# Residual with features on partitions from the output projection to gate and up, and cross attention as one pipeline

## The chip, the core and the metric

The kernel runs on one core of a Trainium2 chip. The metric is the time of one execution on the device, in microseconds (us). Before the change the median of 3 runs is 2864.52 us (2863.82 to 2865.51).

## What is computed

One transformer block in float32 on 2048 tokens of 1024 features, with three kinds of causal attention side by side, cross attention to a memory of 256 tokens, and a gated feed-forward layer:

```python
def _rmsnorm(x, g):
    xf = x.astype(jnp.float32)
    y = xf * lax.rsqrt(jnp.mean(xf * xf, axis=-1, keepdims=True) + EPS)
    return (y * g.astype(jnp.float32)).astype(x.dtype)
...
        y = jnp.concatenate([_rmsnorm(ya, ga), _rmsnorm(yb, gb), _rmsnorm(yc, gc)], axis=-1)
        x = x + y @ w_o[l]
        x = x + _cross(_rmsnorm(x, norm_cross[l]), _rmsnorm(mem, norm_mem[l]),
                       w_cq[l], w_ckv[l], w_co[l])
        h = _rmsnorm(x, norm_ffn[l])
        gate, up = jnp.split(h @ w_gu[l], 2, axis=-1)
        x = x + (jax.nn.silu(gate) * up) @ w_down[l]
```

`_cross` makes queries (4 heads of 128) from the normalised residual, scores them against the memory's keys, takes the softmax, and projects the weighted values back with w_co. The hidden width of the feed-forward layer is 2816, that is 22 blocks of 128.

## The kernel before

The program runs its stages one after the other: projections, the three attentions, output projection, cross attention, gate and up, down projection. Every operand of a large matmul is split into a high and a low part (tiles with h and l at the end), and one product is three matmuls, high by high, high by low and low by high (`mm3`, the matmul is on line 94). The instructions are written by a program whose scheduler puts those of each engine into a fixed order by a simulated timeline when the kernel is built; every engine then runs its own list strictly in that order, and a waiting instruction holds back all behind it. ScalarE's list also issues DMA transfers, as does SyncE's.

The residual lies with tokens on partitions. TensorE multiplies along the partitions, so an operand that is to be summed over features has to be transposed first (by matmuls with an identity matrix, four 128x128 pieces into one PSUM tile); ScalarE then evacuates the high part and VectorE the low part.

- The output projection (lines 889 to 957) goes over 8 pieces of 256 tokens. `load_y` loads two tiles `yt` of 128 tokens of the attention result over ScalarE's queue (line 923), normalises them into `yht` (`rms_rows`, squares on line 119), and transposes them (`transpose_split`: line 142 on TensorE, 146 on ScalarE, 147 on VectorE). w_o is loaded in 8 blocks over SyncE's queue and cast (lines 907 to 909). Per 128 tokens the residual piece is stored to `s_x2`, and normalised to `s_h2` (16 tiles each).
- Cross attention (lines 960 to 1065) loads `s_h2` in four chunks of 512 tokens and transposes it (128 transposes, line 142, tile `ht`). For each chunk and head come queries `cq`, scores and softmax `soft` (tiles `cs`, `cp`), the weighted values `val`, and `outp` (tile `co`), which adds to the residual, stores it to `s_x3`, normalises it and stores that to `s_h3`. The softmax of the next head runs beside the values of the one before; a chunk's `outp` runs inside the next chunk.
- Gate and up (lines 1071 to 1246) uses a seven-product scheme for 2x2 block matrices, in two halves of 1024 tokens by 22 blocks of hidden width. `blocks` forms sums of the operands on GpSimd, and `turn` (lines 1127 to 1129) transposes the 7 x 4 operands of a half: 112 transposes for each half, 224 in all. Weight sums and splits (lines 1158 to 1161, 1103 and 1104) run for each of the 22 blocks.

The pools of the three stages are separate, in SBUF and in PSUM.

Of the kernel before, what the change touches and what calls it, by code (L numbers as in the profile page):

```python
# [8 lines left out]
F32 = mybir.dt.float32  # L9
# [24 lines left out]
def kernel(ctx: ExitStack, tc: tile.TileContext, a: dict, out: bass.AP, dbg=None):  # L34
# [26 lines left out]
    s_x2 = [scratch([CH, D], f"s_x2_{c}") for c in range(NCH)]  # L61
    s_x3 = [scratch([CH, D], f"s_x3_{c}") for c in range(NCH)]
    s_h2 = [scratch([CH, D], f"s_h2_{c}") for c in range(NCH)]
    s_h3 = [scratch([CH, D], f"s_h3_{c}") for c in range(NCH)]
# [15 lines left out]
    G_MIX, G_OUT, G_CROSS, G_MEM, G_Q, G_KV = 0, 8, 16, 24, 32, 34  # L80
# [807 lines left out]
    late = ExitStack()  # L888
    mp = pool(late, "mkv", side="right")
    wqp = pool(late, "cwq", side="right")  # L890

    mp.tile([P, 24], F32, name="rpad")
    mkT = [mp.tile([P, 4, MEM], F32R, name=f"mkT{i}") for i in range(2)]
    mv = [mp.tile([P, 2, 512], F32R, name=f"mv{i}") for i in range(2)]
    with ExitStack() as es:
        xp = pool(es, "ox")
        wp = pool(es, "ow")
        hp = pool(es, "oh")
        rp = pool(es, "or")
        pp = pool(es, "opp", space=PSUM)  # L900

        def loadw(src, tag, bufs, k):
            n = src.shape[1]
            th = wp.tile([P, n], F32R, name="wh_", tag=tag + "h", bufs=bufs)
            tl = wp.tile([P, n], F32R, name="wl_", tag=tag + "l", bufs=bufs)
            r = wp.tile([P, n], F32, name="wraw", tag="wraw", bufs=2)
            nc.sync.dma_start(r, src)
            nc.vector.tensor_copy(th, r)
            (nc.gpsimd if k % 2 else nc.vector).tensor_sub(tl, r, f32(th))
            return th, tl  # L910

        def load_wq(k):
            th, tl = wqp.tile([P, 512], F32R, name=f"wqh{k}"), wqp.tile([P, 512], F32R, name=f"wql{k}")
            r = wp.tile([P, 512], F32, name="wraw", tag="wraw", bufs=2)
            nc.scalar.dma_start(r, a["w_cq"][0][k * P:(k + 1) * P, :])
            split(r, th, tl)
            return th, tl

        def load_y(c):
            hts = []  # L920
            for t in range(2):
                yt = xp.tile([P, D], F32, name="yt", tag="yt", bufs=3)
                nc.scalar.dma_start(yt, s_y[c // 2][(c % 2) * 256 + t * P:(c % 2) * 256 + (t + 1) * P, :])
                ht = xp.tile([P, D], F32, name="yht", tag="ht", bufs=4)
                rms_rows(yt, [(0, 512), (512, 768), (768, 1024)], ht, sp)
                hts.append(ht)
            return transpose_split(hts, G_OUT, hp, pp, "yT", 16, pbufs=2)

        y0 = load_y(0)
        wo = [loadw(a["w_o"][0][k * P:(k + 1) * P, :], "wo", 8, k) for k in range(KT)]  # L930
        yT = {0: y0}
        wq = []
        for c in range(8):
            hh, hl = yT.pop(c)
            if c + 1 < 8:
                yT[c + 1] = load_y(c + 1)
            if c == 3:
                for i in range(2):
                    nc.sync.dma_start(f32(mkT[i]), s_ck[i])
                    nc.sync.dma_start(f32(mv[i]), s_cv[i])  # L940
            if c >= 4:
                wq += [load_wq(2 * c - 8), load_wq(2 * c - 7)]
            for t in range(2):
                ts = slice(t * P, (t + 1) * P)
                r0 = c * 256 + t * P
                rr = slice(r0 % CH, r0 % CH + P)
                xt = rp.tile([P, D], F32, name="xt", tag="xt", bufs=3)
# [12 lines left out]
    with ExitStack() as es:  # L960
# [15 lines left out]
        def turn(hts):  # L976
            return transpose_split(hts, G_CROSS, hp, pp, "xT", 8)
# [468 lines left out]
```

## Time and profile before

| | |
|---|---|
| median of 3 runs | 2864.52 us |
| profiled execution | 2859.2 us |
| its span in the trace | 2857.5 us |
| TensorE, mean granted clock | .988 of full speed |
| output projection, about | 1008 to 1207 us |
| cross attention, about | 1207 to 1484 us |
| gate and up, about | 1484 to 2385 us |

The span is the time between the first and the last instruction in the trace, and the execution's own time is 1.7 us longer. Engines are named PE (TensorE), DVE (VectorE), ACT (ScalarE), POOL (GpSimd) and SP (SyncE); PEld is TensorE's weight load, which overlaps the matmuls. "Busy" of TensorE is a sum over pipelined matmuls whose ends are modelled, so a mean duration is no pitch: the pitch is a stretch of time divided by the matmuls in it.

### The profile page before, as it was taken

What the parts mean: (1) busy time and instruction counts of PE and PEld (TensorE: products, weight loads), DVE (VectorE), ACT (ScalarE), POOL (GpSimd) and SP (SyncE); (2) the same over time, 40 slices, a digit from 0 to 9 for tenths busy, and PEclk for the clock granted to TensorE, in tenths of its full rate; (3) what the DMA queues carried; (4) which work ended last, traced back from release to release, by engine and by line L of the source; (5) the groups of instructions that cost most, each with busy time, mean ns of one, the idle gap of its engine ahead of it and who ended that gap; (6) DMA issues with size and microseconds to landing.
All of it is one profiled execution on the core that took longest, in us unless ns stands there. A gap on an engine that the chain in (4) does not pass through costs nothing. (4 is left out here: it accounts for less than half of the span.)

```text
span 2857.5 us, 40439 instructions
## 1 busy us (share of the span) xinstructions
PE 2762.3 (97%) x13537; PEld 2290.1 (80%) x13537; DVE 1860.7 (65%) x3677; ACT 1306.7 (46%) x2816; POOL 1239.6 (43%) x991
## 2 busy tenths in 40 slices
PE   8999999999999999999989999999999997999996
PEld 7888888888888878778867888887788885888885
DVE  6446458887777764456666665566666663677778
ACT  5225219998776734344444333334333334333335
POOL 3132253332111120010026766666666667579854
PEclk9999999999999999999999999999999998999998
DMA  7755457433342174533253333233333333445434
GB/s 260 261 174 210 177 198 214 123 105 113 114 121 74 50 254 169 181 115 133 97 213 123 110 104 103 90 106 105 108 106 109 100 104 118 130 155 184 133 96 144
DMA packets 300448, 398.72 MB, mean 140 GB/s; under 512 B 39168, under 2 KB 174592, under 8 KB 300240
## 3 DMA queue, kind: packets, MB, share of 16 engines
q1 hardware_dynamic: 291168, 372.79, 39.5%
q10 hardware_dynamic: 9072, 23.35, 2.2%
q8 instruction: 107, 1.75, 0.2%
q14 instruction: 101, 0.83, 0.1%
HBM read 258.54 MB, written 137.51 MB: 139 GB/s over the span
## 5 line engine op out<-in xcount | busy, mean ns | idle before, releaser
L1375 DVE TENSOR_TENSOR acc<-dn,acc 128x512 f32<-128x512 f32 x352 | 226.0, 682 | 69.6 <-PE dn L1368 67.4
L772 POOL TENSOR_TENSOR ptl<-pf,pth 128x512 fp32r<-128x512 f32 (+3 forms) x111 | 109.9, 990 | 361.7 <-ACT pth L771 237.3
L1368 PE MATMUL dn<-wdh,gdh 128*128 128x512 f32 x616 | 238.0, 394 | 18.9 <-ACT acc L1373 15.8
L1104 POOL TENSOR_TENSOR awl<-s,awh 128x512 fp32r<-128x512 f32 x132 | 193.6, 1467 | 131.9 <-ACT awh L1103 123.5
L1368 PE MATMUL dn<-wdl,gdh 128*128 128x512 f32 x616 | 240.4, 391 | 1.2 <-POOL wdl L1267 1.2
L1368 PE MATMUL dn<-wdh,gdl 128*128 128x512 f32 x616 | 236.5, 393 | 3.4 <-POOL gdl L1267 3.4
L1103 ACT CAST awh<-s 128x512 fp32r<-128x512 f32 x176 | 109.1, 621 | 251.5 <-PE p L94 246.9
L723 ACT ACTIVATE pt<-pt,m 128x640 f32<-128x640 f32 (+4 forms) x192 | 206.1, 1076 | 32.9 <-DVE pt L709 29.6
L763 PE MATMUL tp<-ident,pt 128*128 128x128 f32 x1368 | 217.5, 274 | 3.7 <-ACT pt L723 2.3
L775 DVE TENSOR_TENSOR ptl<-tp,pth 128x512 fp32r<-128x512 f32 (+3 forms) x321 | 183.2, 587 | 43.4 <-ACT pth L774 41.2
L1265 ACT CAST gdh<-graw 128x512 fp32r<-128x512 f32 x154 | 95.5, 622 | 247.9 <-PE dn L1368 128.2
L763 PEld LDWEIGHTS tp<-ident,pt 128*128 128x128 f32 x1368 | 165.5, 140 | 30.7 <-ACT pt L723 3.2
L774 ACT CAST pth<-tp 128x512 fp32r<-128x512 f32 (+3 forms) x321 | 159.4, 518 | 43.2 <-PE tp L763 39.7
L1267 POOL TENSOR_TENSOR gdl<-graw,gdh 128x512 fp32r<-128x512 f32 x98 | 137.2, 1412 | 77.9 <-ACT gdh L1265 54.8
L789 PE MATMUL pv<-ptl,va 128*128 128x512 f32 (+3 forms) x432 | 166.2, 391 | 0.0
L703 PE MATMUL s<-ka,qa 128*128 128x512 f32 (+8 forms) x432 | 162.7, 380 | 1.9 <-DVE r L561 0.6
L789 PE MATMUL pv<-pth,va 128*128 128x512 f32 (+3 forms) x432 | 160.6, 374 | 1.9 <-ACT pth L774 1.9
L1103 ACT CAST awh<-graw 128x512 fp32r<-128x512 f32 x132 | 81.5, 619 | 166.4 <-PE p L94 107.9
L1368 PEld LDWEIGHTS dn<-wdh,gdh 128*128 128x128 f32 x616 | 116.6, 189 | 48.1 <-ACT acc L1373 17.6
L1368 PEld LDWEIGHTS dn<-wdh,gdl 128*128 128x128 f32 x616 | 116.7, 190 | 28.3 <-POOL gdl L1267 3.8
L1368 PEld LDWEIGHTS dn<-wdl,gdh 128*128 128x128 f32 x616 | 116.4, 189 | 25.3 <-POOL wdl L1267 1.6
L187 POOL TENSOR_TENSOR wl<-wr,wh 128x512 fp32r<-128x512 f32 (+1 forms) x36 | 50.5, 1405 | 135.2 <-DVE wh L185 112.2
(470 smaller groups left out, 8331.9 us busy)
## 6 DMA issues: line engine op xcount, KB each, us to landing
graw<-in_w_gu_dram SPq DMA_DIRECT2D x88, 512.0 KB
graw<-s_g SPq DMA_DIRECT2D x154, 256.0 KB
s_g<-pair SPq DMA_DIRECT2D x66, 256.0 KB
s_h<-xh SPq DMA_DIRECT2D x32, 512.0 KB
ht<-s_h SPq DMA_DIRECT2D x32, 512.0 KB
wr<-in_w_in_dram SPq DMA_DIRECT2D x48, 256.0 KB
s_g<-u SPq DMA_DIRECT2D x44, 256.0 KB
draw<-in_w_down_dram SPq DMA_DIRECT2D x22, 512.0 KB
```

The costliest lines, as they stand in the source:

```text
L703: nc.tensor.matmul(dst, l, r, start=j == 0, stop=j == len(seq) - 1)
L723: nc.scalar.activation(v.pt[:, 0:nk * P], v.pt[:, 0:nk * P], AF.Exp, bias=v.prev, scale=-1.0, accum_out=u.l[:, t:t + 1])
L763: nc.tensor.transpose(ps[:, t * P:(t + 1) * P], u.p[t][:, o:o + P], ident)
L772: nc.gpsimd.tensor_sub(lo[:, cs], pf[:, cs], f32(hi[:, cs]))
L774: nc.scalar.copy(hi[:, cs], ps[:, cs])
L775: nc.vector.tensor_sub(lo[:, cs], ps[:, cs], f32(hi[:, cs]))
L789: nc.tensor.matmul(st.ps[:, cs], l, r[:, cs], start=b == blocks[0] and j == 0, stop=b == blocks[-1] and j == len(seq) - 1)
L1103: nc.scalar.copy(tiles[0], raw)
L1104: (nc.gpsimd if k else nc.vector).tensor_sub(tiles[1], raw, f32(tiles[0]))
L1267: (nc.vector if cnt[0] % 3 == 0 else nc.gpsimd).tensor_sub(t[1], x, f32(t[0]))
L1368: nc.tensor.matmul(ps[t], l[:, ts], r, start=p == chain[0][0] and i == 0, stop=i == len(seq) - 1, skip_group_check=True)
L1375: nc.vector.tensor_add(x, ps[t], x)
```

## The change

The residual now lies with features on partitions (tiles of 128 features by 512 tokens) from the output projection to gate and up.

- Output projection: w_o is the stationary operand and the transposed attention result the moving one. It goes over four chunks of 512 tokens; all 16 blocks of w_o stay in SBUF. The residual's own input is read from `xT`, the transposed input. The squares of the new residual are summed on ScalarE and GpSimd (`squares`), turned into a sum per token by four matmuls with one column of ones (`rms_cols`), and used as a scale on the scores (`rsc`); norm_cross is folded into w_cq (`load_wq`). There is no `s_h2` any more. In the last chunk `x_steps(0)` reloads the first chunk and splits it.
- Cross attention: one loop over 16 units (chunk and head), with the queries of the next unit and the values of the last inside it. `x_steps` splits the reloaded residual without a transpose (copy on ScalarE, subtraction on VectorE or GpSimd). `outp` writes 128 features at a time. `rows` transposes the new residual back to tokens on partitions for `s_x3` (128 transposes). `norm1` and `norm2` spread the factor of each token over the partitions (four matmuls of `ones` with a diagonal tile `dg`), and multiply (8 operations on VectorE per chunk); the result is stored to `s_h3` with features on partitions.
- Gate and up: `turn` has no transposes: copy on ScalarE, subtraction on VectorE (every fourth on GpSimd), from SBUF. The first two products of the first block are started before the last chunk's norm (`begun`).
- The three stages share one PSUM pool (6 buffers for sums, 2 for transposes).

The diff, cut to its core:

```diff
+    def squares(st, p, m, x):
+        if m == 0:
+            st[0] = p.tile([P, CH], F32, name="ssum", tag="ssum", bufs=1)
+            nc.scalar.activation(st[0], x, AF.Square)
+        else:
+            sq = p.tile([P, CH], F32, name="sq", tag="sq", bufs=2)
+            nc.scalar.activation(sq, x, AF.Square)
+            nc.gpsimd.tensor_add(st[0], st[0], sq)
+
+    def rms_cols(st):
+        ps = pp.tile([P, CH], F32, name="rc", tag="tp", bufs=2)
+        for t in range(4):
+            nc.tensor.matmul(ps[:, t:t + 1], st[0][:, t * P:(t + 1) * P], ones[:, 0:1], start=True, stop=True)
...
+    def x_steps(c, p, tag, bufs):
...
+            nc.sync.dma_start(raw, s_x2[c][k])
+            th, tl = ft()
+            nc.scalar.copy(th, raw)
+            (nc.gpsimd if k % 3 == 1 else nc.vector).tensor_sub(tl, raw, f32(th))
...
         def load_wq(k):
...
+            nc.sync.dma_start(r, a["w_cq"][0][k * P:(k + 1) * P, :])
+            g = gains[:, G_CROSS + k:G_CROSS + k + 1]
+            nc.scalar.mul(th, r, g)
+            nc.vector.scalar_tensor_tensor(out=tl, in0=r, scalar=g, in1=f32(th), op0=ALU.mult, op1=ALU.subtract)
...
         def load_y(c):
             hts = []
-            for t in range(2):
-                yt = xp.tile([P, D], F32, name="yt", tag="yt", bufs=3)
...
+            for t in range(4):
+                yt = xp.tile([P, D], F32, name="yt", tag="yt", bufs=5)
+                nc.scalar.dma_start(yt, s_y[c][t * P:(t + 1) * P, :])
+                junk = xp.tile([P, D], BF16, name="junk", tag="junk", bufs=1)
+                rms_rows(yt, [(0, 512), (512, 768), (768, 1024)], yt, sp, junk=junk)
+                hts.append(yt)
...
+                    for i in range(4):
+                        ms = slice(i * P, (i + 1) * P)
+                        mm3(ps[i], [((wo[k, n][0][:, ms], wo[k, n][1][:, ms]), y[k])], start=k == 0, stop=k == KT - 1)
...
+                for i in range(4):
+                    nc.vector.tensor_add(xt[i], ps[i], xt[i])
+                    nc.sync.dma_start(s_x2[c][4 * n + i], xt[i])
+                    squares(st, rp, 4 * n + i, xt[i])
...
+    def norm2(c, x3, dg):
+        ps = pp.tile([P, CH], F32, name="tp", tag="tp", bufs=2)
+        for t in range(4):
+            nc.tensor.matmul(ps[:, t * P:(t + 1) * P], ones, dg[:, t, :], start=True, stop=True)
+        rb = lp.tile([P, CH], F32, name="rb", tag="sq", bufs=2)
+        nc.scalar.copy(rb, ps)
+        for m in range(KT):
+            nc.vector.scalar_tensor_tensor(out=x3[m], in0=x3[m], scalar=gains[:, G_FFN + m:G_FFN + m + 1], in1=rb,
+                                           op0=ALU.mult, op1=ALU.mult)
+            nc.sync.dma_start(s_h3[c][m], x3[m])
...
+    for u in range(16):
+        c, h = divmod(u, 4)
...
+            def turn(n, raw):
                 B[n] = [bt(n, j) for j in range(4)]
                 for j in range(4):
-                    ps = pp.tile([P, CH], F32, name="tp", tag="tp", bufs=2)
-                    for t in range(4):
-                        nc.tensor.transpose(ps[:, t * P:(t + 1) * P], rows[t][:, j * P:(j + 1) * P], ident)
-                    nc.scalar.copy(B[n][j][0], ps)
-                    nc.vector.tensor_sub(B[n][j][1], ps, f32(B[n][j][0]))
+                    nc.scalar.copy(B[n][j][0], raw[j])
+                    (nc.gpsimd if j % 4 == 3 else nc.vector).tensor_sub(B[n][j][1], raw[j], f32(B[n][j][0]))
...
+        for m in range(KT):
+            outp(3, oT, m, x3, st)
+            if m:
+                rows(3, m - 1, x3)
+            if m % 2 == 0 and begin:
+                begin.pop(0)()
+        begun = [w0, acc(), acc()]
+        block(begun[1], w0[0], B["11"])
+        rows(3, 7, x3)
+        dg = norm1(st)
+        block(begun[2], w0[1], B["t1"])
+        norm2(3, x3, dg)
```

What this does to the order of the instructions is shown at two places. The first is ScalarE at the end of attention and the start of the output projection, before; `pth` and `osb` belong to attention, `yt` are the loads, `trh` the evacuated operands:

```order
L923 DMA yt_13112<-s_y0_124 128x1024
L774 CAST pth_12845<-tp_12843 128x128
L923 DMA yt_13134<-s_y0_124 128x1024
L923 DMA yt_13260<-s_y0_124 128x1024
...
L119 ACTIVATE yht_13114,rms_ss_13115<-yt_13112 128x512
...
L771 CAST pth_13044<-tp_13042 128x128
L109 ACTIVATE rms_rs_13289<-rms_rs_13289 128x3
L794 COPY osb_13068<-pv_12931 128x512
L923 DMA yt_13732<-s_y1_125 128x1024
L146 ACTIVATE trh_13159<-tr_ps_13156,gains_315 128x256
```

The same place with the change (`fth` are the evacuated operands, `wqh` the scaled parts of w_cq):

```order
L770 CAST pth_13096<-tp_13094 128x128
L970 DMA yt_13174<-s_y0_124 128x1024
L970 DMA yt_13196<-s_y0_124 128x1024
L970 DMA yt_13218<-s_y0_124 128x1024
L793 COPY osb_13120<-pv_12983 128x512
L970 DMA yt_13240<-s_y0_124 128x1024
L118 ACTIVATE junk_13176,rms_ss_13177<-yt_13174 128x512
...
L118 ACTIVATE junk_13396,rms_ss_13397<-yt_13394 128x512
...
L982 ACTIVATE fth_13273<-tp_13268,gains_367 128x512
...
L962 ACTIVATE wqh0_14388<-wraw_14390,gains_367 128x512
```

The four loads of the first chunk moved from in front of attention's last casts to behind the last of them, and the squares of five tiles now stand between that cast and the first evacuated operand.

The second place is VectorE at the start of gate and up, before; `xh` is the last chunk's normalised residual, `b` tiles are the operands of the products:

```order
L1038 SCALAR_TENSOR_TENSOR xh_17538<-x3_17507,rms_rs_17541,hgain_15203 128x1024
L1033 TENSOR_TENSOR x3_17552<-co_17568,x3_17552 128x512
L107 TENSOR_SCALAR rms_nt_17587<-rms_ss_17584 128x1
L1129 TENSOR_TENSOR b11_0l_17653<-tp_17660,b11_0h_17652 128x512
L1129 TENSOR_TENSOR b11_1l_17655<-tp_17667,b11_1h_17654 128x512
...
L1038 SCALAR_TENSOR_TENSOR xh_17583<-x3_17552,rms_rs_17586,hgain_15203 128x1024
L1129 TENSOR_TENSOR b11_2l_17657<-tp_17674,b11_2h_17656 128x512
```

The same place with the change (`s1` to `s4` are weight sums of the second block, `rb` the spread factor):

```order
L1098 TENSOR_TENSOR x3_17792<-mm_17794,x3_17792 128x512
L1258 TENSOR_TENSOR s1_18077<-graw_18075 128x512
...
L1261 TENSOR_TENSOR s4_18080<-graw_18073,s2_18078 128x512
L924 COPY rms_ss_17846<-rc_17841 128x4
...
L1116 TENSOR_SCALAR dg_17857<-ident_357,rms_rs_17848 128x128 x4
L1126 SCALAR_TENSOR_TENSOR x3_17568<-x3_17568,gains_367,rb_17879 128x512
...
L1126 SCALAR_TENSOR_TENSOR x3_17792<-x3_17792,gains_367,rb_17879 128x512
L1230 TENSOR_TENSOR b21_0l_17907<-ht_17500,b21_0h_17906 128x512
L1230 TENSOR_TENSOR b21_1l_17909<-ht_17502,b21_1h_17908 128x512
```

The operands of the first two products (`b11`, `bt1`) moved in front of the last residual addition; those of the third (`b21`) stand behind the whole norm, and read SBUF (`ht`) where they read PSUM (`tp`) before.

## Rows read from the trace of the kernel before

**Rows 1.** Page, busy time of each engine, share of the span and instructions:

```profile
PE 2762.3 (97%) x13537; PEld 2290.1 (80%) x13537; DVE 1860.7 (65%) x3677; ACT 1306.7 (46%) x2816; POOL 1239.6 (43%) x991
```

**Rows 2.** Stretches: length, busy (instructions) of PE, PEld, DVE, ACT, POOL; clock; DMA share; GB/s:

```profile
1008.30:1206.80 198.50, 192.96 (x902) 156.01 (x902) 105.82 (x297) 73.70 (x241) 19.97 (x12) 1.00 0.54 196
1206.80:1484.20 277.40, 263.79 (x1313) 214.01 (x1312) 174.75 (x449) 117.92 (x296) 23.95 (x14) 0.97 0.40 146
1484.20:1600.00 115.80, 109.47 (x519) 86.17 (x518) 76.58 (x93) 47.44 (x84) 77.28 (x55) 1.00 0.34 119
1700.00:1815.80 115.80, 115.80 (x500) 93.85 (x500) 70.22 (x77) 38.40 (x65) 75.32 (x54) 1.00 0.32 103
1900.00:2015.80 115.80, 112.45 (x530) 90.22 (x529) 78.00 (x89) 45.47 (x80) 76.57 (x56) 0.99 0.32 108
```

**Rows 3.** The last three stretches, matmuls of line 94 alone:

```profile
1484.20:1600.00 115.80, 101.12 (x405) 73.84 (x404) 1.00 0.34 119
1700.00:1815.80 115.80, 115.80 (x500) 93.85 (x500) 1.00 0.32 103
1900.00:2015.80 115.80, 104.34 (x420) 77.58 (x419) 0.99 0.32 108
```

**Rows 4.** A stretch of the output projection: matmuls (L94), then transposes (L142):

```profile
1100.00:1200.00 100.00, 100.00 (x404) 72.88 (x403) 1.00 0.48 176
...
1100.00:1200.00 100.00, 12.92 (x68) 9.55 (x68) 1.00 0.48 176
```

**Rows 5.** Timeline of ScalarE and its DMA queue: start, length, instruction, [wait before]:

```profile
983.49 0.33 ACTq L923 DMA_DIRECT2D yt<-s_y  x1
...
987.34 0.63 ACT L119 ACTIVATE yht<-yt 128x512 f32<-128x512 f32 x1
...
988.67 0.19 ACT L119 ACTIVATION_READ_ACCUMULATOR yht<-yt 128x1 f32 x1
...
992.08 0.66 ACT L106 ACTIVATE rms_rs<-rms_ss,epsc 128x1 f32<-128x1 f32 x3
...
995.33 0.22 ACT L109 ACTIVATE rms_rs<-rms_rs 128x3 f32<-128x3 f32 x1
...
998.54 0.33 ACTq L923 DMA_DIRECT2D yt<-s_y  x1
...
1003.80 0.64 ACT L119 ACTIVATE yht<-yt 128x512 f32<-128x512 f32 x1 [2.20 <-DMA yt<-s_y]
...
1007.05 0.28 ACT L771 CAST pth<-tp 128x128 fp32r<-128x128 f32 x1
...
1008.37 0.59 ACT L794 COPY osb<-pv 128x512 f32<-128x512 f32 x1 [0.94 <-PE pv L789]
```

**Rows 6.** The stretch of the first matmuls of the output projection:

```profile
1010.00:1020.00 10.00, 8.09 (x39) 5.84 (x38) 6.30 (x12) 3.23 (x8) 2.40 (x1) 1.00 0.98 351
```

**Rows 7.** Timeline of TensorE, first matmuls of the output projection:

```profile
1011.14 1.17 PE L94 MATMUL mm<-wh__13212,trh 128*128 128x512 f32 x4 [1.04 <-DVE wh__13212 L908]
```

**Rows 8.** Stretches behind a pause of TensorE, columns as in rows 2:

```profile
1223.40:1226.80 3.40, 2.82 (x9) 2.43 (x10) 0.79 (x2) 0.53 (x1) 2.31 (x1) 0.50 1.04 406
1450.00:1500.00 50.00, 41.49 (x175) 30.44 (x173) 36.17 (x69) 18.91 (x42) 17.42 (x14) 0.86 0.46 160
```

**Rows 9.** Waits of TensorE in cross attention: total, times, longest:

```profile
PE cq L94 <- DVE trl L147: 3.2, 1, 3.2
PE cq L94 <- ACT trh L146: 2.4, 1, 2.4
```

**Rows 10.** VectorE by line in cross attention: busy, mean ns, idle before:

```profile
L155 DVE CAST wch<-wraw 128x1024 fp32r<-128x1024 f32 x4 | 4.7, 1226 | 2.0 <-DMA wraw<-in_w_co_dram 2.0
```

**Rows 11.** VectorE by line, 1484.2 to 1600:

```profile
L1104 DVE TENSOR_TENSOR awl<-graw,awh 128x512 fp32r<-128x512 f32 x9 | 10.3, 1154 | 0.0
...
L1219 DVE TENSOR_TENSOR pair<-pair,u 128x512 f32<-128x512 f32 x2 | 3.6, 1777 | 0.0
...
L1129 DVE TENSOR_TENSOR bt_0l<-tp,bt_0h 128x512 fp32r<-128x512 f32 x4 | 2.7, 687 | 1.3 <-ACT bt_0h L1128 1.3
```

More of the change, by code (lines that the diff above doesn't have):

```diff
@@ L885 @@
             f()
[L888 to L892, printed above, removed]
+    mid = ExitStack()
+    pp = pool(mid, "mpp", space=PSUM)
+    cp = pool(mid, "mc")
+    ones = cp.tile([P, P], F32, name="ones")
+    nc.gpsimd.memset(ones, 1.0)
+    nc.scalar.dma_start(gains[:, G_FFN:G_FFN + KT], a["norm_ffn"].rearrange("o (k p) -> p (o k)", p=P))
+    right = ExitStack()
+    wqp = pool(right, "cwq", side="right")
@@ L895 @@
     with ExitStack() as es:
+        wp = pool(es, "ow")
         xp = pool(es, "ox")
[L897 to L898 removed]
         rp = pool(es, "or")
[L900 to L907, printed above, removed]
+        wo = {}
@@ new lines, in outp, with rows @@
+    def outp(c, oT, m, x3, st):
+        ms = slice(m * P, (m + 1) * P)
+        x = lp.tile([P, CH], F32, name="x3", tag="x3", bufs=9)
+        nc.sync.dma_start(x, s_x2[c][m])
+        ps = pp.tile([P, CH], F32, name="mm", tag="mm", bufs=6)
+        mm3(ps, [((wc[h][0][:, ms], wc[h][1][:, ms]), oT[h]) for h in range(4)])
+        nc.vector.tensor_add(x, ps, x)
+        squares(st, lp, m, x)
+        x3.append(x)
+    def rows(c, m, x3):
+        ps = pp.tile([P, CH], F32, name="tp", tag="tp", bufs=2)
+        for t in range(4):
+            nc.tensor.transpose(ps[:, t * P:(t + 1) * P], x3[m][:, t * P:(t + 1) * P], ident)
+        xs = lp.tile([P, 4, P], F32, name="xs", tag="xs", bufs=2)
+        nc.scalar.copy(xs, ps.rearrange("p (t n) -> p t n", n=P))
+        nc.sync.dma_start(s_x3[c][:, m * P:(m + 1) * P].rearrange("(t p) n -> p t n", p=P), xs)
@@ new lines, with load_wc @@
+    wc = []
+    def load_wc(k):
+        th, tl = wp.tile([P, D], F32R, name=f"wch{k}"), wp.tile([P, D], F32R, name=f"wcl{k}")
+        for n in range(2):
+            r = lp.tile([P, CH], F32, name="wraw", tag="x3", bufs=9)
+            nc.sync.dma_start(r, a["w_co"][0][k * P:(k + 1) * P, n * 512:(n + 1) * 512])
+            split(r, th[:, n * 512:(n + 1) * 512], tl[:, n * 512:(n + 1) * 512])
+        wc.append((th, tl))
+    q = cq(0, y)
+    pts = None
+    oT, ready = [], None
+    fill = []
@@ L1242 @@
                     nB, nafter = blocks(load_h(2), load_h(3))
+                    nafter["p0"]()
                 if f == NF - 1 and half == 0:
                     after = nafter
-                gated(half, f, B, after)
+                first = half == 0 and f == 0
+                gated(half, f, B, ahead if first else after, begun if first else None)
             B = nB
+    mid.close()
     with ExitStack() as es:
```

427 lines of the change are left out of this document (223 added, 204 removed).

## The prediction

> **What bounds the kernel now.** I read the page's shares first: TensorE is busy 97% of the span, VectorE, the next, 65% [rows 1]. So a transpose that leaves TensorE is worth its pitch, and a wait is worth its length, unless something fills it. Then I read the span by stage [rows 2]. The reader should see there that the stretches which the change touches are the ones with idle TensorE: 5.5 us of 198.5 in the output projection, 13.6 of 277.4 in cross attention, 6.3 of 115.8 at the start of gate and up, 3.4 of 115.8 where its second half begins, and none in a steady stretch of the same length. The same three stretches counted in matmuls alone [rows 3] say more: 500 in the steady one, so **.2316 us** a matmul; 405 and 420 in the other two, so 95 and 80 matmuls, or 22.0 and 18.5 us, are lost there. Some 112 transposes each explain part of it: the output projection fits 404 matmuls and 68 transposes into 100 us without a pause [rows 4], so a transpose costs (100 - 404 x .2316)/68, about .1 us, and 112 cost 11. The rest, 11 and 7, is waiting.
>
> **TensorE's account.** Removed: 128 transposes of the normalised residual in cross attention and 224 in gate and up, 352 x .1 = 35 us. Added: 128 that turn the new residual back into rows, 13 us, and 48 small norm matmuls (16 one-column ones for the first norm, 32 for the second), some 4 us by estimate. That alone is **-18 us**. The matmul count stays. What remains is what TensorE waits for, stage by stage.
>
> **Output projection: +15.** Today the four loads of the attention result that its first matmuls need are issued well ahead: the first at 983.49 and used at 987.34, the next used 1003.80 [rows 5], while attention runs on to 1008.37, where its last result is copied. In the changed order (first two fences) all four stand on ScalarE behind the last cast of attention, which starts here at 1007.05 [rows 5], and a fifth load's squares come before the first operand is evacuated. Nothing covers this: TensorE's next instruction needs the first tile. The price: from issue to use, 5.3 us (998.54 to 1003.80) or at most 3.9 (983.49 to 987.34) [rows 5]. Squares take 1.4 us a tile (987.34 to about 988.8), the three logarithms .7 and the exponential .2, so 2.3, and five tiles 11.5. From 1007.3 that is 1007.3 + 3.9 or 5.3 + 11.5 + .7 for the first operand, 1023.4 to 1024.8. The DMA engines were 98% busy at 351 GB/s in that place already [rows 6]; four tiles of 512 KB take 6 us with all of it and 12 with half, which would put the last tile at 1021 to 1022 and the first matmul near 1027. Today it runs at 1011.14 [rows 7]. So 12 to 16 later; I take 14.5. After a pause TensorE was at half clock for 3.4 us at 1223.4 (granted .50), and for about 14 us around 1455 (.86 over 50 us, so .14 x 50 at half) [rows 8]; I take 2.5. The norm matmuls add 1. From this I take off 3: 198.5 less 768 x .2316 and 128 x .1 leaves 7.8 us lost today, of which 5 come after the first matmul and most should go with all of w_o resident. The eight scalings of w_cq that now stand in ScalarE's queue between the third and the sixth operand I cost at nothing: three operands give TensorE 36 x .2316 = 8.3 us of work, against 4 x .62 of scaling before the fourth. If their loads come late, that cover is gone. SyncE's queue now carries the residual in 256 KB pieces, stored, loaded twice and stored again, and the second copy of it, normalised, is gone; with the DMA engines at .54 and .40 in these stages [rows 2] I cost that at nothing, unless a load is queued behind a store that waits.
>
> **Cross attention: -9.** Pure work today is 864 x .2316 + 192 half-wide matmuls at half that + 256 x .1 = 248 us of 277.4, so 29 are lost: the clock's .03 of the stretch, 8 us [rows 2], and waits for the two halves of operands at the first unit and smaller ones [rows 9]. Afterwards the work is 128 + 128 transposes and the norm matmuls, 251. The first unit's operands are prepared inside the output projection, so its two waits (3.2 and 2.4) go. Late next: VectorE's casts of w_co stand before the first softmax, as long as today's (4.7 us of work that waits for its loads [rows 10]), of which I count 4; at each of three chunk ends eight multiplications of the FFN norm stand in VectorE's queue between two score evictions, with 27 matmuls (6 us) as cover, some 2 each; 4 at the last unit, which has no successor; and 3 for the clock. That is 17 for 29, less 3 of added matmuls: -9 (bounds -16 and -2).
>
> **Start of gate and up: -5.** Now 22 lost. After the change two products run before the last norm is done, 24 matmuls and 20 transposes, 7.6 us. Behind the last residual block, VectorE holds, in this order (third and fourth fence): four weight sums, the norm, eight multiplications, and only then the operand of the third product. The chain is an addition .7, a square .6, GpSimd's sum 1.4 (its 77 us in 55 instructions [rows 2]), the norm about 4 with its small matmuls and a copy, eight multiplications at about .95 (between .69 and 1.2), and the subtraction 1.15: 15.4. So 8 us idle. Then fifteen subtractions at 1.15, 17.3 us, feed five products of 13.9 us: 3.4, plus 3 for other VectorE work in between and 2.5 of half clock. **17 for 22** (bounds 10 and 28).
>
> The price of these subtractions is the term that I doubt most. Today they read PSUM and take 687 ns. Afterwards both inputs are in SBUF, like today's weight subtractions in the same stretch, which average 1154 for nine, and up to 1777 for the sums of the gated pairs [rows 11], while GpSimd is busy 77 us of 115.8 [rows 2]. I take 1.15, the mean of the nearest row.
>
> **Second half: -4.5.** Now 18.5 lost. In the last product group of the first half VectorE has 21 such subtractions, 24 us, and about 15 us of its usual work, 39 against 84 x .2316 = 19.5; some 5 can start early. 14 for 18.5 (bounds 5 and 30).
>
> **Sum.** +15 - 9 - 5 - 4.5 = -3.5 against the profiled execution of 2859.2, so 2855.7; the median of runs is 5.3 higher, so **2861**. About 5.7 us (0.2%) is what a measurement tells from no change, so this is no change.
>
> **Rivals.** *TensorE's account holds* (chance .28): the waits hardly grow. Out +10, cross -16, start -12, second half -13: -31, 2833. For it: TensorE at 97%. Against: the queue order, which no load can pass. *The subtractions run as slowly as the slowest row* (.13): SBUF operations at 1.78 in place of 1.15, for 15 + 21 subtractions and 8 multiplications, add 44 x .63 = 28, so 2889. It decides for slower from about 1.36 each (44 x .21 = 9). For it: GpSimd gets a quarter of the subtractions and so is busier. Against: the mean of today's row. The Trainium skill's SBUF — State Buffer (Terms) says that VectorE and GpSimd take their shared port pair exclusively for a whole instruction, the loser blocking; each would then wait out one GpSimd operation. By that rule a subtraction would be an estimated 2.1 us and the time about 2903; the 1154 measured says the collision is partial here. *The loads come later still* (.15): the w_o and residual loads compete with the four tiles, and the w_cq scalings hold ScalarE; the pause is 27 and not 15, so 2873.
>
> **Chances.** My own case has .44, with about ±9 around 2861: faster .17, same .16, slower .11. The first rival gives .27 and .01; the second .13 slower; the third .09 slower, .06 same. So faster **.44**, same **.23**, slower **.33**. Leaving out part of the first rival and the top of the second gives 2837 to 2884; my own case alone is 2852 to 2870.
>
> **What would show it.** A pause of TensorE of 12 us or more before the first matmul of the output projection, ended by the loads or the first evacuated operand; no long pause at cross attention's first unit; a pause of 5 to 10 us at the third product, ended by a VectorE subtraction; such subtractions at 1.0 to 1.3 us on average; some 425 matmuls in the first 115.8 us of gate and up. A pause under 6 at the output projection, or subtractions near .7, makes it wrong towards faster; subtractions over 1.5, towards slower.

## The result and the profile after

The changed kernel takes 2881.42 us (median of 4 runs, 2877.74 to 2881.91) where the kernel before took 2864.78 on the same chip (2863.82 to 2865.51). The ratio is 1.0057, with an interval of 1.0044 to 1.0071: slower by .57%, 16.6 us, and more than the .2% that a measurement tells from no change. The forecast was 2861, no change; 2881 lies inside the range (2837 to 2884), but the time moved, and the other way from the -3.5 of the sum.

The profiled execution took 2877.7 us with a span of 2876.0, 18.5 more than before. Page of the changed kernel, busy time of each engine, as in [rows 1]:

```profile
PE 2735.9 (95%) x13409; PEld 2289.7 (80%) x13409; DVE 1863.5 (65%) x3555; ACT 1314.0 (46%) x2780; POOL 1367.2 (48%) x1074
```

TensorE is busy 26 us less and the span is 18.5 longer: it waits more. GpSimd has 128 us more work. The same stretches as in [rows 2], moved with the stages (output projection, cross attention, the start of gate and up, a steady stretch, the start of its second half):

```profile
1009.40:1222.50 213.10, 197.49 (x924) 162.35 (x925) 92.77 (x245) 83.10 (x242) 38.34 (x29) 0.94 0.43 147
1222.50:1502.80 280.30, 262.74 (x1350) 218.82 (x1350) 169.32 (x395) 122.61 (x297) 78.62 (x59) 0.98 0.42 134
1502.80:1618.60 115.80, 94.97 (x401) 76.11 (x400) 81.96 (x93) 46.27 (x83) 93.48 (x59) 0.90 0.40 125
1700.00:1815.80 115.80, 115.80 (x512) 95.91 (x512) 72.27 (x81) 39.85 (x68) 78.10 (x54) 1.00 0.32 103
1920.00:2035.80 115.80, 100.37 (x406) 80.81 (x405) 87.63 (x84) 45.84 (x82) 88.98 (x60) 0.91 0.26 84
```

And the large matmuls alone in the third of these, as in [rows 3] (the two others hold nothing else):

```profile
1502.80:1618.60 115.80, 88.98 (x365) 70.72 (x366) 0.90 0.40 125
```

By stage, after less before: the output projection 213.1 for 198.5, **+14.6**; cross attention 280.3 for 277.4, **+2.9**; the start of gate and up holds 365 matmuls where the steady stretch holds 512, so 147 x .2262 = 33.3 us are lost for 22.0, **+11.3**; the second half loses 106 x .2262 = 24.0 for 18.5, **+5.5**. The steady stretch itself has become quicker: 512 matmuls for 500, .2262 us for .2316, and gate and up has 44 x 84 = 3696 of them, **-20**. Attention ends 1 us later, and the down projection, of which the prediction says nothing, is 5.5 longer (478.1 us from the last matmul of gate and up to the end, for 472.6). The sum is some 21 for the 18.5 measured.

**Output projection.** ScalarE and its DMA queue:

```profile
1005.83 0.27 ACT L770 CAST pth<-tp 128x128 fp32r<-128x128 f32 x1
1005.89 1.87 ACTq L970 DMA_DIRECT2D yt<-s_y  x3
...
1012.23 0.63 ACT L118 ACTIVATE junk<-yt 128x512 bf16<-128x512 f32 x1 [2.26 <-DMA yt<-s_y]
```

TensorE there:

```profile
1017.50 0.69 PE L979 MATMUL tp<-ident,yt 128*128 128x128 f32 x2 [6.35 <-DVE yt L124]
...
1027.63 0.69 PE L979 MATMUL tp<-ident,yt 128*128 128x128 f32 x2 [4.66 <-DVE yt L124]
1028.88 2.93 PE L93 MATMUL mm<-fth,woh 128*128 128x512 f32 x6 [0.56 <-ACT fth L982]
```

The loads are issued .06 us after attention's last cast, as the order said; the first squares start 6.3 us later, and the first matmul 17.7 us later than in [rows 7].

**Cross attention.** The longest of its pauses stands at the end of the third chunk. TensorE, then VectorE, then GpSimd in that place:

```profile
1474.56 0.77 PE L1122 MATMUL tp<-dg,ones 128*128 128x128 f32 x2 [7.88 <-DVE dg L1116]
```

```profile
1466.08 5.25 DVE L1068 TENSOR_SCALAR cp<-cp,cl 128x256 f32<-128x256 f32 x4
1471.26 1.22 DVE L109 TENSOR_TENSOR rms_nt<-rms_nt,rms_rs 128x4 f32<-128x4 f32 x1
...
1473.93 0.16 DVE L1113 TENSOR_TENSOR rms_rs<-rms_rs,rms_nt 128x4 f32<-128x4 f32 x1
```

```profile
1466.09 1.28 POOL L1224 TENSOR_TENSOR ht<-ht 128x512 f32<-128x512 f32 x1
1467.32 2.60 POOL L1223 TENSOR_TENSOR t<-ht 128x512 f32<-128x512 f32 x2
1469.88 3.80 POOL L1224 TENSOR_TENSOR ht<-ht 128x512 f32<-128x512 f32 x3
```

The reader should lay the last two beside each other. The four divisions of the scores take 1.31 us each, which is one GpSimd sum each (1.27 to 1.30); an operation on 4 elements of each partition takes 1.22 while the sums run and .16 once they are over, at 1473.68. The sums (`sums0`, lines 1223 and 1224) are operand work of gate and up that the scheduler has put beside the last chunk of cross attention.

A second wait stands at the first unit, where TensorE sums the squares of the output projection's last chunk and waits for GpSimd (total, times, longest):

```profile
PE rc L922 <- POOL ssum L916: 2.9, 1, 2.9
```

The two waits for operands that the first unit had before [rows 9] are gone.

**Start of gate and up.** Waits of TensorE in the third stretch (total, times, longest):

```profile
PE mm L93 <- DVE b_0l L1230: 4.7, 1, 4.7
PE rc L922 <- POOL ssum L916: 3.5, 1, 3.5
PE mm L93 <- POOL b_3l L1230: 3.4, 1, 3.4
PE tp L1106 <- ACT xs L1108: 2.6, 2, 2.3
PE mm L93 <- POOL awl L1209: 2.2, 1, 2.2
PE tp L1122 <- DVE dg L1116: 2.0, 1, 2.0
```

The third product waits for the subtraction, as predicted, but 3.5 us of waiting stand before it for GpSimd's sum of squares and 3.4 behind it for GpSimd's quarter of the subtractions. The cause of the latter, in GpSimd's timeline (the first of two sums that stand before its subtraction `b_3l`, which starts at 1540.30):

```profile
1531.44 7.67 POOL L1240 TENSOR_TENSOR ht<-ht 128x512 f32<-128x512 f32 x1 [12.78 <-DVE b_0l L1230]
```

and VectorE's at the same time, the first and the last of twelve subtractions back to back:

```profile
1530.68 0.68 DVE L1230 TENSOR_TENSOR b_0l<-ht,b_0h 128x512 fp32r<-128x512 f32 x1
...
1537.30 0.68 DVE L1230 TENSOR_TENSOR b_2l<-ht,b_2h 128x512 fp32r<-128x512 f32 x1
```

Here VectorE runs at .68 each and it is GpSimd that stands: one sum takes 7.67 us, where others take 1.27, and ends 1.1 us after the last of VectorE's twelve. So the two engines hold each other up in both directions. The Trainium skill's SBUF — State Buffer (Who interferes with whom) says that a VectorE operation with two SBUF inputs, or a tensor-scalar one in a two-port mode, and a GpSimd operation that reads SBUF contend for a shared port pair, and that whoever issues first has it for the whole instruction while the other blocks. The trace agrees in the first place, with 1.31 us against 1.27 to 1.30. In the second it shows more than one instruction: the sum was held for the whole run of VectorE operations that followed each other without a gap.

**Second half.** Line 1230 there, VectorE's part (columns as in the stretches): at the start 16 subtractions in 12.73 us, .80 each; here 21 in 27.8, 1.32 each.

```profile
1502.80:1618.60 115.80, 12.73 (x16) 7.69 (x5) 0.90 0.40 125
1920.00:2035.80 115.80, 27.80 (x21) 12.10 (x7) 0.91 0.26 84
```

TensorE's waits in the second of these, all for VectorE:

```profile
PE mm L93 <- DVE awl L1209: 7.8, 3, 4.6
PE mm L93 <- DVE u L1309: 4.7, 1, 4.7
PE mm L93 <- DVE u L1303: 3.0, 1, 3.0
```

Most of the rest is the clock: granted .91 here, and .99 in the same place before [rows 2]. In this piece TensorE does not wait at all and gets 16 matmuls into 5 us, where 22 fit at 1.00 (length, busy of PE, clock, DMA share, GB/s):

```profile
2000.00:2005.00 5.00, 5.00 (x16) 0.67 0.00 0
```

At .91, some 20 of the 115.8 us were at half clock; 37 matmuls began in them, some .43 apart for .2262, which makes about 7 us by estimate.

**Down projection.** ScalarE behind the last product of gate and up (its last matmul is at 2397.91), then TensorE:

```profile
2411.65 0.62 ACT L1390 CAST wdh<-draw 128x512 fp32r<-128x512 f32 x1 [14.68 <-DMA draw<-in_w_down_dram]
```

```profile
2415.21 0.79 PE L1493 MATMUL dn<-wdh,gdh 128*128 128x512 f32 x1 [16.91 <-ACT gdh L1390]
```

Before, TensorE's first product began 1.1 us behind the last of gate and up (2386.03 behind 2384.92); it paused there too, but after a part of its work:

```profile
PE dn L1368 <- ACT acc L1373: 15.8, 3, 14.8
```

### The profile page after: what moved, and what is told of

Its sections match the earlier page's. It is cut to its first block, busy times and chain, and to the rows that moved or that the text cites. A ratio compares the mean times of both kernels' runs of the same rounds, so it can differ in the third digit from the quotient of the medians.

```text
span 2876.0 us, 40455 instructions
## 1 busy us (share of the span) xinstructions
PE 2735.9 (95%) x13409; PEld 2289.7 (80%) x13409; DVE 1863.5 (65%) x3555; ACT 1314.0 (46%) x2780; POOL 1367.2 (48%) x1074
## 5 line engine op out<-in xcount | busy, mean ns | idle before, releaser
L1209 POOL TENSOR_TENSOR awl<-s,awh 128x512 fp32r<-128x512 f32 x132 | 206.6, 1565 | 86.9 <-ACT awh L1208 86.9
L916 POOL TENSOR_TENSOR ssum<-ssum,sq 128x512 f32<-128x512 f32 x56 | 75.3, 1345 | 295.3 <-ACT sq L915 253.2
```

Of the source, the lines that this page charges most:

```text
L1209: (nc.gpsimd if k else nc.vector).tensor_sub(tiles[1], raw, f32(tiles[0]))
```

## The experiments

Differences are between medians. The kernel before, run beside each experiment, had medians from 2862.7 to 2864.8 us; by the ratios to it, experiments 1, 2 and 4 give back 6, 4 and 19 us where the times say 7, 6 and 21.

**1. The down projection's loads.** The pool for its loads lies over temporaries of gate and up that are in use to the end; the edit puts it at the other end of SBUF.

```diff
-        rp = pool(es, "dr")
+        rp = pool(es, "dr", side="right")
```

> The raw tiles of the down projection (pool dr) are put on the other side of SBUF, where gate and up kept its operands that are read by the last time in the middle of the stage. Theory: in the changed kernel these tiles lie over the temporaries of gate and up, which are in use to its end, so that the loads of w_down are issued only at 2408, 10 us after the last matmul of gate and up; with the other place they are issued earlier, the 17.3 us pause before the first matmul of the down projection shrinks to under 8, and the time falls by 5 to 12 us against the changed kernel (2881 to between 2869 and 2876). Rival: the first matmul waits for the gated products that come back through DRAM, which are stored at 2398 to 2404 whatever w_down does; then the pause only moves behind the first matmuls, as in the kernel before (15.2 us at 2398.7), and the time stays within 3 us.

2874.06 us, 1.0035 (1.0022 to 1.0048): -7, as the theory said, but the first matmul still waits 12.8 us, where it was to be under 8. The weights are loaded in time; their cast now stands in ScalarE's queue behind casts of the gated products, and those wait for the products that are stored last and loaded again (ScalarE, then TensorE):

```profile
2416.16 1.95 ACT L1390 CAST gdh<-graw 128x512 fp32r<-128x512 f32 x3 [8.63 <-DMA graw<-s_g]
2419.47 0.62 ACT L1390 CAST wdh<-draw 128x512 fp32r<-128x512 f32 x1 [1.36 <-DMA s_g<-pair]
2420.14 2.08 PE L1493 MATMUL dn<-wdh,gdh 128*128 128x512 f32 x4 [12.84 <-ACT wdh L1390]
```

So the place of that pool made the loss of this stage: it takes 466.7 us for 478.1. The edit has a price elsewhere, which number 8 shows: the loads are now issued in the middle of gate and up (the first at 1991.27), and GpSimd's sums of w_down come with them.

**2. The output projection's loads.** Two pools change places, so that the loaded tiles lie where attention has done with its own earlier.

```diff
-        wp = pool(es, "ow")
         xp = pool(es, "ox")
+        wp = pool(es, "ow")
```

> Only the order in which two SBUF pools of the output projection are opened is swapped, so that the tiles of the attention result (yt) lie where the kernel before had them and w_o lies above. Theory: the loads stood behind the last cast of attention because their place was taken by tiles that this cast's transposes read; now they stand some 50 instructions earlier in ScalarE's queue, the pauses between 1010 and 1029 (16.4 us in five pieces) shrink to under 6, and the time falls by 9 to 16 us. Rival: w_o, now in the place that comes free last, is late in its turn, and TensorE waits for its casts in place of the tiles; then the first matmul comes no earlier than 6 us before 1028.9 and the time falls by less than 6.

2875.1 us, 1.0042 (1.0027 to 1.0057): -6, less than the 9 to 16 of the theory, though the first matmul comes 16 us earlier, which rules out the rival. The loads are issued 20 us earlier and the first matmul runs at 1012.80 instead of 1028.88:

```profile
985.59 0.33 ACTq L970 DMA_DIRECT2D yt<-s_y  x1
```

```profile
1012.80 0.73 PE L93 MATMUL mm<-fth,woh 128*128 128x512 f32 x2 [0.34 <-ACT fth L982]
...
1018.55 1.12 PE L979 MATMUL tp<-ident,yt 128*128 128x128 f32 x4 [3.54 <-DVE ftl L983]
```

The 16 us come back as 8 in the stage (213 to 205): TensorE then waits for the next operands, prepared one by one. The mechanism of the prediction is shown, its undoing is worth about half of its price.

**3. The squares' sums on VectorE.**

```diff
-            nc.gpsimd.tensor_add(st[0], st[0], sq)
+            nc.vector.tensor_add(st[0], st[0], sq)
```

> The 56 additions that collect the squares of the residual move from GpSimd to VectorE, and nothing else. Theory: GpSimd's queue is what the norms wait for (3.3 us at 1227.9, 3.7 at 1515), and its operations hold up VectorE's own SBUF operations; without them both pauses go to under 1.5 each, VectorE's contended operations in cross attention get shorter, and the time falls by 4 to 9 us. Rival: VectorE is the engine that TensorE waits for, and 56 more operations of .68 us (38 us) in its queue lengthen those waits; then the time rises by 2 to 10 us.

2880.85 us, 1.0063 (1.0046 to 1.008): no change, neither the theory's 4 to 9 less nor the rival's 2 to 10 more. The wait for the sum at the start of gate and up falls from 3.5 to 1.4, and others take its place: the longest wait for `dg` grows from 7.9 to 8.7, that for `cp` from 2.1 to 3.4. The sum has only moved from one queue to the other.

**4. The operand work of gate and up on VectorE alone**, sums and subtractions (five lines, of which two are shown).

```diff
-                    nc.gpsimd.tensor_sub(t3[j], b22[j], b12[j])
+                    nc.vector.tensor_sub(t3[j], b22[j], b12[j])
...
-                    (nc.gpsimd if j % 4 == 3 else nc.vector).tensor_sub(B[n][j][1], raw[j], f32(B[n][j][0]))
+                    nc.vector.tensor_sub(B[n][j][1], raw[j], f32(B[n][j][0]))
```

> In gate and up all sums and all subtractions that make the operands go to VectorE: 23 operations of each half leave GpSimd. Theory: the two engines do not read SBUF side by side but take turns, so that a GpSimd operation of 1.3 to 1.7 us costs VectorE about as long as it lasts; VectorE's operations fall to about .7 us and the excess of the two transitions does not grow: the time falls by 2 to 12 us. Rival: GpSimd works in parallel, and VectorE, which TensorE waits for there, gets 23 x .68 = 16 us more in each half: the time rises by 10 to 30 us.

2860.21 us, .9991 (.9981 to 1.0): **-21**, the whole loss, though VectorE has more to do, and more than the 2 to 12 of the theory. The four divisions and the sums that GpSimd could not get through:

```profile
1466.87 1.14 DVE L1068 TENSOR_SCALAR cp<-cp,cl 128x256 f32<-128x256 f32 x4
```

```profile
L1240 DVE TENSOR_TENSOR ht<-ht 128x512 f32<-128x512 f32 x4 | 2.8, 690 | 0.0
```

1.14 us for 5.25, and .69 us a sum of line 1240 for 2.99 on average. The subtractions of line 1230, now all on VectorE, take .72 on average at the start (20 in 14.32 us) and .88 in the second half (28 in 24.64), for .80 and 1.32. Large matmuls at the start (this run's stage begins at 1500.5) and in the second half:

```profile
1500.50:1616.30 115.80, 95.08 (x397) 75.55 (x396) 0.91 0.43 137
1920.00:2035.80 115.80, 106.32 (x452) 85.55 (x451) 0.97 0.27 85
```

397 for 365 and 452 for 406: 7 and 10 us. The pause at the third chunk's end falls only from 7.9 to 6.3, because the sums now stand in VectorE's own queue there. The run does not separate two things: the collisions are fewer, and a sum is shorter on VectorE (.69) than on GpSimd even where nothing slows it (1.27).

**5. The division of the scores on ScalarE**, which takes the slowed operations away and leaves the sums that slow them.

```diff
-            nc.vector.tensor_scalar_mul(pt[:, t, :], pt[:, t, :], l[:, t:t + 1])
+            nc.scalar.mul(pt[:, t, :], pt[:, t, :], l[:, t:t + 1])
```

> In the changed kernel's cross attention the division of the scores by their sum (64 operations, SBUF to SBUF, line 1068) moves from VectorE to ScalarE. Theory: the 8.2 us pause at 1466.4 comes from GpSimd's operand sums for gate and up, beside which these four operations took 5.25 us in place of about 1.2; without them VectorE reaches the norm earlier and the pause falls to 3 to 5 us, though the norm's own small operations still wait for GpSimd; the time falls by 2 to 6 us. Rival: the norm waits for GpSimd's sum of squares or for ScalarE; then the pause stays above 7.

2882.03 us, 1.0062 (1.0042 to 1.0083): no change. The pause is 6.2 us for 7.9, between theory (3 to 5) and rival (above 7): the sums now slow what comes next. VectorE:

```profile
1473.38 2.87 DVE L1116 TENSOR_SCALAR dg<-ident,rms_rs 128x128 f32<-128x128 f32 x4
```

2.87 us, where the same four took .87 behind the sums.

**6. The pitch: weights moved by 128 bytes.** In the built programs (no view of the traces shows addresses) the high and low parts of the weights begin at 128 modulo 256 bytes of a partition in both kernels; the operands that are multiplied with them begin at 0 before and at 128 after. The edit adds an unused tile of 128 bytes, and the weights begin at 0.

```diff
+        hp.tile([P, 32], F32, name="pad2")
```

> The changed kernel with one unused tile of 128 bytes per partition added in gate and up, which moves the weight tiles there (pool fw) by 128 bytes and no operand. In the changed kernel weights and operands start at the same byte address modulo 256 (128 and 128), in the kernel before at different ones (128 and 0). Theory: this alone sets the pitch of a matmul in the steady stretch, 226.8 ns in the changed kernel against 232.4 before; the steady pitch of gate and up goes from 19.04 to about 19.5 us per block of 84 matmuls, and the time rises by 15 to 22 us. Rival: the pitch comes from something else in the change (the common PSUM pool, the missing transposes); then it stays at 226.8 ns and the time within 4 us.

2901.73 us, 1.0126 (1.0102 to 1.015): **+20**, as the theory said. The steady stretch, large matmuls:

```profile
1700.00:1815.80 115.80, 115.80 (x498) 93.16 (x497) 1.00 0.31 100
```

498 for 512: the pitch of the kernel before is back.

**7. The kernel before with its weights moved by 128 bytes**, so that weights and operands both begin at 0.

```diff
-        gp.tile([P, 24], F32, name="pad")
+        gp.tile([P, 56], F32, name="pad")
```

> The kernel before, with its own unused tile in gate and up made 128 bytes longer, so that weights and operands there start at the same address modulo 256 (0 and 0). Theory: the steady pitch falls from 232.4 to about 227 ns, and the time of the kernel before by 15 to 22 us (to about 2842 to 2848), without anything else of the change. Rival: the pitch stays, and the time within 4 us.

2846.5 us, .9935 (.991 to .9959): **-18**, as the theory said. The steady stretch:

```profile
1700.00:1815.80 115.80, 115.80 (x513) 95.88 (x512) 1.00 0.33 106
```

With 6 this settles it: one pad takes either kernel from its own pitch to the other's. The quicker pitch is no work of the new layout. At equal pitch the change costs 2881.4 - 2846.5 = 35 us.

**8. Edits 1, 2 and 4 together**, and w_cq moved so that it begins at 128 as its operands do (it began at 224).

```diff
+    rpp = pool(right, "rp0", side="right")
+    rpp.tile([P, 24], F32, name="rpad")
...
-    wqp.tile([P, 24], F32, name="rpad")
```

> Together: operand sums and subtractions on VectorE, the attention result's tiles below w_o, the down projection's raw tiles on the other side, and w_cq moved by 96 bytes so that it and its operands start at the same address modulo 256. If the parts add up (-21, -6, -7 measured alone, and 384 matmuls x 6.5 ns = -2.5 for w_cq): about 2845, and below the kernel before by 0.5% or more. Rival: the parts meet the same waits (the start of the down projection waits for the gated products, the pause moves), so that less than two thirds add up: 2854 or more.

2845.11 us, .993 (.9908 to .9952): 36 us less than the changed kernel. The parts make 7 + 6 + 21 = 34, and w_cq some 2 (its 384 matmuls began .2289 us apart for .2336; it was not run alone). So the savings add up, within what the intervals resolve. The longest waits up to the start of gate and up that are left:

```profile
PE tp L1123 <- DVE dg L1117: 8.4, 2, 6.3
PE tp L980 <- DVE ftl L984: 4.9, 2, 3.5
```

Here edit 1 shows its price. The first 252 matmuls of gate and up's second half, in number 4 and then in this run:

```profile
1945.90:2016.30 70.40, 60.97 (x253) 48.34 (x252) 55.95 (x62) 22.99 (x40) 52.32 (x34) 0.95 0.31 100
1940.30:2017.40 77.10, 63.06 (x253) 50.04 (x252) 55.75 (x62) 22.91 (x40) 60.79 (x40) 0.91 0.39 129
```

GpSimd has six operations more, the sums of w_down, and the stretch is 6.7 us longer (77.7 us in number 10, which has both edits too). Without edit 4 it is 77.9 us in number 1 and 74.4 in the changed kernel (72.9 to 76.1 in numbers 2, 3, 5 and 11). Which of the early work costs this, the loads or the sums, no run separates.

This version is 19 us quicker than the kernel before, and number 7 is 18: the change with four edits gains no more than the kernel before with one unused tile.

**9. The kernel of 7 with its operand sums on VectorE**, to see whether edit 4 helps without the change (four lines of this kind).

```diff
-                nc.gpsimd.tensor_sub(x, h2[t][:, hi], h2[t][:, lo])
+                nc.vector.tensor_sub(x, h2[t][:, hi], h2[t][:, lo])
```

> The kernel before with even addresses (the run before_even), and its 32 operand sums of gate and up moved from GpSimd to VectorE. Its operand subtractions read PSUM, so by the theory that the two engines take turns at SBUF they are not held up by GpSimd, and there is little to win: within 5 us of 2846.5 (against -21 for the same move in the changed kernel, whose subtractions read SBUF). Rival: the -21 of the changed kernel came from GpSimd being the slower engine for this work, wherever the subtractions read; then this kernel wins too, 10 us or more.

2845.06 us, .9931 (.9917 to .9946): 1.4 less than number 7, which is no difference. Where the operands come from PSUM, moving GpSimd's sums wins nothing; so the 21 us of number 4 are a cost that the change brought, not one that was there.

**10. Number 8 with edits 3 and 5 as well.**

> The joined version (2845.1), with the sums of squares moved from GpSimd to VectorE and the division of the scores to ScalarE as well. Alone each of the two changed nothing (2880.9 and 2882.0 against 2881.4). Theory: each pause is then set by the other engine's queue, and with GpSimd out of cross attention and of the last norm the pauses at the last unit (6.5) and before the last norm (3.0) go to under 4.5 and 2: 2838 to 2843. Rival: VectorE's own queue is the bound there; then it stays at 2845 within 3, or rises.

2845.09 us, .9934 (.9916 to .9952): no change against number 8, as the rival said. GpSimd is out of cross attention and of the last norm, and VectorE's own queue is the wait:

```profile
PE tp L1123 <- DVE dg L1117: 6.9, 2, 4.9
```

**11. The changed kernel without the norm of the last chunk.**

```diff
-        dg = norm1(st)
         block(begun[2], w0[1], B["t1"])
-        norm2(3, x3, dg)
+        for m in range(KT):
+            nc.sync.dma_start(s_h3[3][m], x3[m])
```

> The changed kernel, in which the last chunk's residual goes to gate and up without its norm: no sum over partitions, no spreading, no eight multiplications for that chunk (its squares are still formed, its output is stored as it is). It prices the place of this norm, between the second and the third product of gate and up. Theory: of the 33 us lost in the first six blocks of gate and up the pauses between 1512 and 1531 (15.8 us with the half clock behind them) belong to this norm; the time falls by 13 to 20 us. Rival: the third product waits for its operand subtractions and for GpSimd's sums in any case, which take as long without the norm; the time falls by less than 7.

2872.8 us, 1.0029 (1.0016 to 1.0042): -8.6, between theory (13 to 20) and rival (under 7). Of the 33 us lost at the start the norm's chain is about a quarter. Without it TensorE waits for the operands one after the other:

```profile
PE mm L93 <- ACT b_0h L1229: 4.3, 1, 4.3
...
PE mm L93 <- DVE bt_2l L1230: 1.5, 2, 0.7
```

## Why the prediction was right and wrong

In short: the forecast added +15 - 9 - 5 - 4.5. The first term came as said; the three others were +2.9, +11.3 and +5.5, because waits that were to shrink did not, and two terms were missing, one of each sign.

**What bounds the kernel: right. TensorE's account: too good.** Every stage that the change touches got longer or lost more, so the waits decided, as the prediction said against its first rival. In the account the step "48 small norm matmuls, some 4 us" is short: each stands twice in the trace (64 instructions of line 922, 32 of line 1122), which is why TensorE has 128 instructions fewer and not 176. Eight of them take .89 us (up to 1464.84, where the next matmul begins), so 96 take some 11:

```profile
1463.95 1.02 PE L922 MATMUL rc<-ones,ssum 128*128 128x1 f32 x8 [0.31 <-DVE pl L159]
```

The account is about -11 for -18. TensorE is busy 26 us less, but the pitch makes 20 of that, and the half clock, which lengthens what it does, works against it (mean granted .977 for .988).

**Output projection, +15: right, and for the reason given.** +14.6 measured. The loads are issued at 1005.89 for the 1007 assumed, the squares begin 6.3 us later for the 3.9 to 5.3, and five tiles take to 1023. The first matmul at 1028.88 is 1.9 us later than the "near 1027": between, two of VectorE's norm operations on 3 elements of each partition take 1.24 and 1.23 us (at 1023.72 and 1025.89) beside GpSimd's weight subtractions, where those for other tiles take .16. Two errors cancel: 16.6 us are lost before the first matmul for the 14.5 taken, and after it 2.0 are won where the other items (2.5 + 1 - 3) make +.5. Experiment 2 takes away the late loads and the pause before the first matmul with them. It returns 6 to 8 of the 15, so part of the stage's loss is the preparation of all operands from scratch, which the prediction priced with the loads in one sum.

**Cross attention, -9: wrong, +2.9.** The failing step is "17 for 29": against the prediction's own work of 251 us, 280.3 still lose 29. The first unit's two waits went, but 2.9 for GpSimd's sum of squares, which no term has, came in their place. The chunk ends, counted with some 2 us each for multiplications in VectorE's queue, show one pause, 7.9 at the third, and it stands in front of the multiplications: the norm's short operations and the divisions, each held up by a GpSimd sum. In GpSimd's order these sums stand between the squares' sums of the third and the last chunk; I had read the orders of VectorE and ScalarE only. The norm matmuls counted too low are in this stage as well. The rest is in waits of 2.1 and less, which no run takes apart.

**Start of gate and up, -5: wrong, +11.3.** The step that failed is "8 us idle" up to the third product. The pauses there add up to 13.7: 2.3 for a copy of the rows on ScalarE, 3.5 for GpSimd's sum of squares, 2.0 for `dg`, 1.2 for ScalarE's half of the operand, and 4.7 for VectorE's, the one that was announced (as 5 to 10). VectorE's part of the chain was even quicker than priced: eight multiplications in 5.39 us for 7.6, and .68 for the subtraction. The price that I doubted most was not at fault here: 16 subtractions take .80 each for 1.15. What failed is that only VectorE's side of the collision had a price. GpSimd has a quarter of the subtractions, the sums and the squares. Its last sum of squares was priced with 1.4 and no queue, and stood behind a weight subtraction of its own (1515.67); the waits for its quarter and for another weight subtraction (3.4 and 2.2) have no term in the sum. In experiment 4, with the sums and subtractions on VectorE, the stage loses 7 us less. The half clock cost about 5 for the 2.5 counted: nine matmuls from 1531.42 to 1535.42 took .44 each and seven from 1542.77 to 1545.75 took .43, 3.4 us more than at .2262, and the 16 norm matmuls took .21 for .11.

**Second half, -4.5: wrong, +5.5.** The failing step is "14 for 18.5", which was 24. Here the price was low, 1.32 for 1.15, which is 3.6 us on 21 subtractions in VectorE's queue, and TensorE waited for that queue alone. And the clock has no term at all, where it cost about 7. Experiment 4 gives back 10 us here; the granted clock rises to .97 with it.

**Second rival, the subtractions at the slowest row: its mechanism, not its size.** Over both stretches 37 subtractions take 40.5 us, 1.10 each, under the 1.36 from which it was to decide. The Trainium skill's SBUF — State Buffer (Terms), cited with it, describes what the two timelines above show; the 2.1 us a subtraction that were worked out from it were too high, as these took from .68 to 1.78.

**Third rival, the loads later still: no.** The first matmul is 1.9 us behind the forecast, not 12.

**Two terms were missing.** The down projection (+5.5) was never looked at, because no line of it changes; the place of its pool changed with the pools before it, and experiment 1 returns 7. And the pitch of the steady stretch was taken as fixed at .2316; it fell to .2262, which gave 20 us back. That gain is an accident of the addresses (6 and 7). Without it the changed kernel takes 2901.7, outside the range, so that 2881 lies inside it is luck: at equal pitch the change costs 35 us.

**What stays open.** Experiments 2 and 8 leave waits for `ftl` and `dg` that no run here removed, and the price of edit 1 in gate and up is seen and not explained. The stage sums and the span differ by 2 us, which the counts of matmuls do not resolve.

## What to carry to other kernels

Here, moving an operand's source from PSUM to SBUF put VectorE's work in competition with what GpSimd did at that time: price both engines, read both orders, and try giving all of it to VectorE. When a change frees TensorE by some percent, look at each place where the next stage's loads are issued, the stages behind the change too, because pools that move make loads wait for other tiles, and loads that come early bring their work with them. And compare a steady stretch that the change leaves alone: where its pitch differs, part of the result is not the change.

## What the runs showed of the hardware

The pitch of fp32r matmuls of 128x512 depended on where the two operands lie in SBUF: .2316 and .2325 us (500 and 498 in 115.8 us) with the weights and the operands 128 bytes apart modulo 256, .2257 and .2262 (513 and 512) with both at the same place, at 0 or at 128, and at a granted clock of 1.00 in all four. One unused tile of 128 bytes was worth 18 us in one kernel and cost 20 in the other.

w_cq's matmuls, with 224 and 128, took .2336, and .2289 once both were at 128. No other distances were tried.

An operation of VectorE on 4 elements of each partition took 1.22 us beside a GpSimd sum and .16 without; four divisions of 128x256 took 5.25 and 1.14. In the other direction, a GpSimd sum took 7.67 us beside twelve VectorE subtractions without a gap, and 1.27 without them. Subtractions with a PSUM operand took .69 beside such sums [rows 11].
